# Taking a head's mean off the values instead of off the weighted sums in a retention layer

## The chip, the cores and the metric

The kernel runs on one core of a Trainium2 chip. The metric is the device time of one execution in microseconds (us), as the median of several runs. All data are float32; TensorE is mostly fed with float32r operands, where each number is split into a high part (a cast) and a low part (what the cast left), and a product is made of three matmuls (high by high, low by high, high by low).

## The reference

Two layers, each of a half step (a gated feed-forward with RMS norm), a mixer and a second half step, and a final RMS norm. The input has 512 frames of 1024 features. In the mixer one projection feeds three groups: a convolution (256 features), a stick-breaking attention (8 heads of 64) and a retention (4 heads of 64). What matters here is the retention and the norm over each head's features behind it:

```python
def retention(q, k, v):            # (B, S, H, Dh), Dh = 64
    # weight of key s for query t: gamma_h^|t-s| in the own chunk of 64 frames,
    # gamma_h^(t-s) for earlier chunks, 0 for later ones
    ...
    return (y_intra + y_cross).reshape(B, S, H, Dh)

def head_norm(y, g):
    mu = jnp.mean(y, axis=-1, keepdims=True)
    yc = y - mu
    var = jnp.mean(yc * yc, axis=-1, keepdims=True)
    return (yc * lax.rsqrt(var + EPS)).reshape(B, S, H * Dh) * g

y_r = jax.nn.silu(g_r) * head_norm(retention(rotary(q_r), rotary(k_r), v_r), ret_norm_g)
```

The retention is a sum over keys of weight times value, and the weights are the same for all 64 features of a head. So the mean of y over the features is the same sum over the means of the values.

## The kernel before

The frames lie along the free dimension: a tile is 128 features by 512 frames. The program is not emitted as it is written. Each step is added to a plan as an operation with its engine, an estimated cost, and what it reads and writes. The planner (`Plan.forward`, L192) then runs through estimated time: on each engine it takes, of the operations that are ready, the one with the lowest rank, and that gives a fixed order for each engine. The rank is the operation's place in the program plus shifts: `late` arguments, and the tables `SHIFTS`, by the name of the function that adds it and by the engine. `ORDER` sets the places of the mixer's steps in the program: c (the convolution's inputs), g (gates), i0 to i5 (queries and keys of six pairs of heads; i1 and i4 are the retention's), taps (the convolution), vs and vr (values of the attention and of the retention), a0 to a5 (the pairs' sums), e (the convolution's end), o (the first half of the output product). `DENSE_LATE` puts the large products of the mixer behind the attention's small ones, so that they fill gaps; `TAPS_LATE` puts the 62 taps of the convolution (one VectorE instruction each) behind VectorE's other work. `SPLITS` has a letter for each weight tile: v splits it with a cast on ScalarE and a subtraction on VectorE, d loads it twice, the second time with an accumulating DMA that GpSimd issues.

Tiles come from rooms with a fixed count of slots. A strict room hands its slots out in the order in which the program creates the tiles; a loose one allows others. In PSUM there are three banks for products (`mm`, loose), four for scores (`z`, strict) and one for the sums over keys (`y`, strict). `tiny` has six strict slots for the small columns of norms (`room("tiny", 6)`, L1337).

The retention's way through the code: `values` (L874) multiplies the normalised input by the values' weights, a PSUM bank for two row tiles of 128 frames (the reduction in L894 to L896), and splits each row tile into high (ScalarE, L911) and low (VectorE, L915) with the row's norm factor as scale. `ret_head` (L1039) makes scores (`scores`, L939), multiplies by the decays (L1049), splits, and `weighted` (L957) sums over keys on TensorE (L968). `head_norm` (L1103) then subtracts the mean with one float32 matmul by a constant 128x128 matrix (`centre`, L1106), squares (L1108) and copies back (L1109) on ScalarE, sums the squares by head with small matmuls (L1114), takes the inverse root (`inv_sqrt`, L484), spreads it over the features (L1133) and applies it, the gain and the gate (L1138, L1144). `split_y` (L1062) splits the result for the output product; for the first half of that product the casts wait for the last operation of i5 (L1326).

Of the kernel before, what the change touches and what calls it, by code (L numbers as in the profile page):

```python
# [10 lines left out]
ACT = mybir.ActivationFunctionType  # L11
ALU = mybir.AluOpType
PSUM = bass.MemoryType.PSUM

P = 128
S = 512
# [18 lines left out]
HOLD = 6  # L35


ORDER = "c g i0 taps vs i1 vr a0 a1 i2 i3 a2 i4 a3 a4 i5 a5 e o".split()
SQUARES_LATE = 80

KINDS = "0mffmfe"

SHIFTS = {
    "m": {
        "attend/tensor": -1700, "conv/vector": 505, "inputs": -505, "parts/vector": 5, "ret_head/vector": 80,
        "twice": -10, "twice/vector": 2230, "weight/scalar": 1450, "weight/vector": -10, "weight_by_dma": 410,
        "weights": -3320, "x_ready/scalar": 210,
    },
    "f": {
        "gated/vector": -295, "inner": 435, "inner/tensor": -30, "norm": -180, "parts/scalar": -545,  # L50
        "parts/vector": -1310, "po": -10, "po/tensor": 625, "weight/gpsimd": -430, "x_ready": 395,
    },
    "0": {
        "forms": 1370, "po/tensor": 380, "po/vector": 30, "weight": -1015, "weight/vector": 1300,
        "x_ready/vector": 145,
    },
}


SPLITS = {  # L60
    "0": "vvvvvvvdvvvvvdvdvdvdvvvdvvdvvvvvvdvdvvd",
    "m": "vvdvvvvdvdddvvddvvdvdvvdvdd",
    "f": "dvdvdddddvdvvvddvdvdvdvvvddvvdvvvdvvvvvvdddvvvvddvd",
}

DENSE_LATE, TAPS_LATE = 1140, 1480
PARTS = ((0, 6), (6, 12), (12, 17), (17, 22))
HS = S // 2
TT = S // P
# [280 lines left out]
class Kernel:  # L350
# [520 lines left out]
        return out  # L871

    @group
    def values(self, src, n, cols, out):  # L874

        nc, r = self.nc, self.r
        mm = nc.tensor.matmul
# [22 lines left out]
        for t in range(TT):  # L900
            ps, at = banks[t // share], (t % share) * cols

            for i, tile in enumerate(out[t]):

                def view(tile=tile, ps=ps, at=at + i * HS):
                    parts = tile[:].rearrange("p (h b f) -> p h b f", b=2, f=64)
                    return ps[:, at : at + HS].rearrange("p (h f) -> p h f", f=64), parts[:, :, 0, :], parts[:, :, 1, :]

                def high(t=t, view=view):
                    v, hi, _ = view()  # L910
                    nc.scalar.activation(hi, v, ACT.Copy, scale=r[:, t : t + 1])  # L911

                def low(t=t, view=view):
                    v, hi, lo = view()
                    nc.vector.scalar_tensor_tensor(  # L915
                        out=lo, in0=v, scalar=r[:, t : t + 1], in1=hi.bitcast(F32), op0=ALU.mult, op1=ALU.subtract
                    )

                self.a(HS, high, [ps, r], [(tile, "h")])
                self.v(HS, low, [ps, r, (tile, "h")], [(tile, "l")])  # L920


    BANKS = ((S, ((1, 0), (3, 3 * P))), (2 * P, ((2, 0),)), (S, ((0, 0),)))
# [178 lines left out]
    @group  # L1102
    def head_norm(self, p, y, gain):  # L1103
        nc = self.nc
        ce = self.bank(self.mm, "yce")
        self.pe(0.86, lambda: nc.tensor.matmul(ce[:], self.centre[:], y[:], start=True, stop=True), [self.centre, y], [ce])  # L1106
        sq = self.tile(self.f2, "rsq")
        self.a(S, lambda: nc.scalar.activation(sq[:], ce[:], ACT.Square), [ce], [sq])  # L1108
        self.a(S, lambda: nc.scalar.copy(y[:], ce[:]), [ce], [y])  # L1109
        vs = self.bank(self.mm, "vs")  # L1110

        def sums():
# [156 lines left out]
    def mixer(self, l, after):  # L1269
# [30 lines left out]
        for step in ORDER:  # L1300
            if step[0] in "sa" and self.tables is None:
                self.exp_tables(silus + sigmoids)
            if step == "g":
                silus += self.gates(w_in, banks)
            elif step == "c":
                sigmoids += self.conv_in(w_in, silus, banks)
            elif step == "vs":
                self.vs = [[self.tile(self.r2, "vs", dtype=F32R) for _ in range(2)] for _ in range(TT)]
                self.values(io["m_vs"][l], 2, 512, self.vs)
            elif step == "vr":  # L1310
                self.vr = [[self.tile(self.r2, "vr", dtype=F32R)] for _ in range(TT)]
                self.values(io["m_vr"][l], 4, 256, self.vr)
            elif step[0] == "i":
                self.inputs(int(step[1]), w_in, banks)
                self.last_inputs = len(self.plan.ops) - 1
            elif step[0] == "a":
                self.attend(int(step[1]), rg)
            elif step == "taps":
                self.conv(cw, cb)
            elif step == "o":  # L1320
                self.out_part(w_out, 0)
            elif step == "e":
                self.conv_end(cg, cbeta)
            banks = None
# [6 lines left out]
    def run(self):  # L1331
# [58 lines left out]
            self.v(P, fn, [ones], [t])  # L1390
        self.a(P, lambda: nc.scalar.copy(ident_r[:], ident[:]), [ident], [ident_r])
        self.tri, self.mask = const("tri", [P, P], F32R), const("mask", [P, P], F32R)
        self.blk, self.centre = const("blk", [P, 2]), const("centre", [P, P])
        self.par = {
            n: const(n, [P, DEPTH, *sh])
            for n, sh in (("conv_w", [2, CONV_W]), ("conv_b", [2]), ("conv_ln_g", [2]), ("conv_ln_b", [2]), ("ret_norm_g", [2]))
# [30 lines left out]
def constants():  # L1427
# [6 lines left out]
    diag = np.where(i[:, None] < i[None, :], 0.0, NEG).astype(f)  # L1434
    c["mask"] = diag
    c["blk"] = ((i[:, None] // 64) == (i[None, :] // 64)).astype(f) / f(64)
    c["centre"] = np.eye(P, dtype=f) - c["blk"]
    c["blk"] = np.ascontiguousarray(c["blk"][:, 63:65])
    half = 32
    inv = (f(1.0) / (f(10000.0) ** (np.arange(half, dtype=f) / f(half)))).astype(f)  # L1440
# [61 lines left out]
```

## Time and profile before

| | us |
|---|---|
| median of 3 runs (lowest, highest) | 1919.26 (1919.08, 1924.63) |
| profiled execution | 1922.25 |
| its span, first to last instruction | 1920.5 |
| TensorE busy (matmuls) | 1886.7 |
| VectorE busy | 1325.8 |
| ScalarE busy | 963.0 |
| GpSimd busy | 226.8 |
| DMA, whole span | 301.37 MB |

A profile shows one execution. Busy time of an engine counts its instructions' spans; matmuls overlap each other, so a busy TensorE is not one at its peak. "Granted clock" is the share of full clock that TensorE got. A wait is put down to the instruction that released it last. Tile names appear without their numbers: yce is the centred sum, yr the retention's sum, vr and vs the split values, pv the values' bank, pj a projection's bank, po and mo the output products of a half step and of the mixer, z the scores, y the sums over keys. Mixer 1 runs from about 367 to 614 us, mixer 2 from about 1311 to 1558 us.

### The profile page before, as it was taken

What the parts mean: (1) busy time and instruction counts of PE and PEld (TensorE: products, weight loads), DVE (VectorE), ACT (ScalarE), POOL (GpSimd) and SP (SyncE); (2) the same over time, 40 slices, a digit from 0 to 9 for tenths busy, and PEclk for the clock granted to TensorE, in tenths of its full rate; (3) what the DMA queues carried; (4) which work ended last, traced back from release to release, by engine and by line L of the source; (5) the groups of instructions that cost most, each with busy time, mean ns of one, the idle gap of its engine ahead of it and who ended that gap; (6) DMA issues with size and microseconds to landing.
All of it is one profiled execution on the core that took longest, in us unless ns stands there. A gap on an engine that the chain in (4) does not pass through costs nothing.

```text
span 1920.5 us, 28960 instructions
## 1 busy us (share of the span) xinstructions
PE 1886.7 (98%) x11412; PEld 1683.5 (88%) x11412; DVE 1325.8 (69%) x1921; ACT 963.0 (50%) x1527; POOL 226.8 (12%) x262
## 2 busy tenths in 40 slices
PE   8999999999999999999999999999999999999997
PEld 6899999888878889899889989998888889998995
DVE  6856655699787856566685656657988787564664
ACT  5444444455886534344544444444668765343442
POOL 1011010010102011110211010101111121011100
PEclk9999999999999999999999999999999999999998
DMA  8366675465337577675866676655554385675742
GB/s 249 104 173 180 176 174 155 134 156 139 91 79 197 129 180 193 161 190 161 217 148 163 172 194 170 177 137 142 126 145 121 80 204 138 177 190 154 190 133 79
DMA packets 106344, 301.37 MB, mean 157 GB/s; under 512 B 12384, under 2 KB 13920, under 8 KB 106208
## 3 DMA queue, kind: packets, MB, share of 16 engines
q0 software_dynamic: 43520, 112.74, 30.3%
q1 hardware_dynamic: 62688, 186.78, 30.2%
q8 instruction: 90, 1.47, 0.3%
q14 instruction: 46, 0.38, 0.1%
HBM read 288.98 MB, written 2.10 MB: 152 GB/s over the span
## 4 chain that ended last, share of the span: by engine, by line
PE 82%; DVE 7%; DMA 7%; ACT 2%; issue 1%; SPq 0%; DVEq 0%; POOLq 0%; ACTq 0%
PE po L434 8%; PE po L435 8%; PE po L436 8%; PE pu L662 6%; PE pu L663 6%; PE pu L664 6%; DMA w_raw<-in_f_in 5%; PE pr L663 4%; PE pr L664 4%; PE pr L662 4%; PE pf L434 3%; PE pf L436 3%; PE pf L435 3%; DVE yc L1202 2%; PE pj L434 2%; PE pj L435 2%
## 5 line engine op out<-in xcount | busy, mean ns | idle before, releaser
L379 DVE TENSOR_TENSOR w_lo<-w_raw,w_hi 128x1024 fp32r<-128x1024 f32 (+2 forms) x281 | 313.6, 1117 | 163.8 <-PE po L436 52.4
L376 ACT CAST w_hi<-w_raw 128x1024 fp32r<-128x1024 f32 (+2 forms) x281 | 269.6, 963 | 239.0 <-DVE w_raw L685 69.8
L434 PE MATMUL po<-hh,w_hi 128*128 128x512 f32 x704 | 275.9, 392 | 0.3 <-DVE x L781 0.3
L435 PE MATMUL po<-hl,w_hi 128*128 128x512 f32 x704 | 275.4, 391 | 0.0
L436 PE MATMUL po<-hh,w_lo 128*128 128x512 f32 x704 | 274.0, 389 | 0.0
L662 PE MATMUL pu<-B_hi,w_hi 128*128 128x256 f32 x560 | 158.6, 283 | 4.3 <-DVE up L712 4.3
L662 PE MATMUL pr<-T_hi,s_hi 128*128 128x256 f32 x560 | 157.8, 282 | 0.9 <-ACT ga L699 0.9
L663 PE MATMUL pu<-B_lo,w_hi 128*128 128x256 f32 x560 | 158.4, 283 | 0.0
L664 PE MATMUL pu<-B_hi,w_lo 128*128 128x256 f32 x560 | 158.2, 283 | 0.0
L663 PE MATMUL pr<-T_lo,s_hi 128*128 128x256 f32 x560 | 157.7, 282 | 0.0
L664 PE MATMUL pr<-T_hi,s_lo 128*128 128x256 f32 x560 | 157.6, 281 | 0.0
L436 PEld LDWEIGHTS po<-hh,w_lo 128*128 128x128 f32 x704 | 132.2, 188 | 28.5
L434 PEld LDWEIGHTS po<-hh,w_hi 128*128 128x128 f32 x704 | 132.6, 188 | 24.7 <-DVE x L781 1.2
L677 POOL DMA_DIRECT2D w_raw<-in_f_in x70 | 84.6, 1214 | 583.7 <-DMA w_raw<-in_f_in 418.9
L435 PEld LDWEIGHTS po<-hl,w_hi 128*128 128x128 f32 x704 | 132.7, 188 | 21.9
L404 ACT ACTIVATE w_lo<-w_hi 128x1024 fp32r<-128x1024 f32 (+2 forms) x85 | 79.3, 933 | 96.0 <-DMA w_hi<-in_f_out 30.6
L781 DVE SCALAR_TENSOR_TENSOR x<-po,x 128x512 f32<-128x512 f32 x128 | 87.1, 687 | 51.9 <-PE po L436 51.8
L436 PE MATMUL pf<-xh,w_lo 128*128 128x512 f32 x304 | 118.8, 391 | 0.8 <-DVE w_lo L379 0.8
L434 PE MATMUL pf<-xh,w_hi 128*128 128x512 f32 x304 | 119.5, 393 | 0.0
L435 PE MATMUL pf<-xl,w_hi 128*128 128x512 f32 x304 | 118.7, 390 | 0.0
L725 ACT ACTIVATE ga<-ga 128x512 f32<-128x512 f32 x88 | 55.3, 630 | 121.8 <-DVE ga L719 108.7
L699 ACT COPY ga<-pr 128x256 f32<-128x256 f32 x140 | 51.9, 370 | 125.1 <-PE pr L664 124.7
(216 smaller groups left out, 5037.6 us busy)
## 6 DMA issues: line engine op xcount, KB each, us to landing
w_raw<-in_f_in SPq DMA_DIRECT2D x225, 512.0 KB, 4.7
w_raw<-in_f_in POOLq DMA_DIRECT2D x70, 512.0 KB, 8.0
w_raw<-in_f_out SPq DMA_DIRECT2D x48, 320.0 KB, 3.1
w_raw<-in_f_out SPq DMA_DIRECT2D x38, 384.0 KB, 4.6
w_raw<-in_m_in SPq DMA_DIRECT2D x26, 512.0 KB, 4.4
w_hi<-in_f_out POOLq DMA_DIRECT2D x26, 384.0 KB, 5.2
w_lo<-in_f_out POOLq DMA_DIRECT2D x26, 384.0 KB, 5.0
w_hi<-in_f_in POOLq DMA_DIRECT2D x19, 512.0 KB, 6.0
```

The costliest lines, as they stand in the source:

```text
L376: self.a(n, lambda: nc.scalar.copy(view(hi), view(src)), [src], [hi])
L379: lambda: nc.vector.tensor_tensor(out=view(lo), in0=view(src), in1=view(hi).bitcast(F32), op=ALU.subtract),
L404: self.a(n, lambda: nc.scalar.activation(lo[:, :n], hi[:, :n].bitcast(F32), ACT.Copy, scale=-1.0), [hi], [lo])
L434: mm(acc[:], hi[:, c], h[:], start=first and a + i == 0, stop=False)
L435: mm(acc[:], hi[:, c], l[:], start=False, stop=False)
L436: mm(acc[:], lo[:, c], h[:], start=False, stop=last and a + i == len(ks) - 1)
L662: mm(out, hi[:, c], h, start=first and j + i == 0, stop=False, **opts)
L663: mm(out, hi[:, c], l, start=False, stop=False, **opts)
L664: mm(out, lo[:, c], h, start=False, stop=j + i == 2, **opts)
L677: lambda: nc.gpsimd.dma_start(rs[:].rearrange("p (a b) -> p a b", a=2), src[:, None, 2 * q : 3 * q].to_broadcast([P, 2, q]), accum_op=ALU.add,
L725: self.last_silus = [self.a(S, lambda: nc.scalar.activation(g[:], g[:], ACT.Silu), [g], [g], "silu")]
L781: lambda x=x, po=po: nc.vector.scalar_tensor_tensor(out=x[:], in0=po[:], scalar=-0.5, in1=x[:], op0=ALU.mult, op1=ALU.add),
```

## The change

The centring matmul, its constant and the copy back are gone; the square reads the sum itself. In `values` for the retention, VectorE first sums each head's 64 features of a row tile (four sums a row), and a second instruction adds -1/64 of the sum to the values and writes them to SBUF. The split then reads that tile, where it read PSUM. The sums take a tile of the room `tiny`. With this the order tables change: `ORDER` puts i1 ahead, i0 behind vs and the taps, a2 before i3, i5 before a4, and the output's first half (o) before a5; ranks and splits of weights change in all stages. The letters d go from 10 to 12 of 39 in the first half step, stay 12 of 27 in a mixer, and go from 23 to 20 of 51 in each other half step.

```diff
-ORDER = "c g i0 taps vs i1 vr a0 a1 i2 i3 a2 i4 a3 a4 i5 a5 e o".split()
-SQUARES_LATE = 80
+ORDER = "c g i1 vs taps i0 vr a0 a1 i2 a2 i3 i4 a3 i5 a4 o a5 e".split()
+SQUARES_LATE = 160
...
     "m": {
-        "attend/tensor": -1700, "conv/vector": 505, "inputs": -505, "parts/vector": 5, "ret_head/vector": 80,
-        "twice": -10, "twice/vector": 2230, "weight/scalar": 1450, "weight/vector": -10, "weight_by_dma": 410,
-        "weights": -3320, "x_ready/scalar": 210,
+        "attend": 55, "conv": -50, "conv/vector": 540, "gates": 825, "inputs": -535, "inputs/scalar": -280,
+        "inputs/vector": -210, "out_part": 220, "parts": 450, "parts/scalar": 90, "products/tensor": 340,
+        "project/tensor": 20, "queries": -395, "queries/vector": 390, "spread": 790, "twice/vector": 2385,
+        "values": 175, "weight": -90, "weight_by_dma": 900, "weight_by_dma/scalar": 315, "weights": -2980,
+        "x_ready/scalar": -1075, "x_ready/vector": 280,
     },
     "f": {
-        "gated/vector": -295, "inner": 435, "inner/tensor": -30, "norm": -180, "parts/scalar": -545,
-        "parts/vector": -1310, "po": -10, "po/tensor": 625, "weight/gpsimd": -430, "x_ready": 395,
+        "forms": 100, "gated/vector": -100, "inner": 450, "norm": -970, "parts": -555, "parts/vector": -1070,
+        "po/tensor": 635, "spread/vector": -200, "weight": -970, "weight/scalar": -470, "weight_by_dma": 915,
+        "x_ready": 410,
     },
     "0": {
-        "forms": 1370, "po/tensor": 380, "po/vector": 30, "weight": -1015, "weight/vector": 1300,
-        "x_ready/vector": 145,
+        "first_weights/sync": 530, "forms": 1455, "gate/vector": 1655, "inner/sync": 615, "inner/vector": -590,
+        "norm/tensor": -1565, "parts/scalar": -30, "parts/vector": -915, "pf": 205, "pf/sync": -310, "po": 410,
+        "x_ready": 75,
     },
...
-DENSE_LATE, TAPS_LATE = 1140, 1480
+DENSE_LATE, TAPS_LATE = 960, 1300
...
-    def values(self, src, n, cols, out):
+    def values(self, src, n, cols, out, centred=False):
...
             for i, tile in enumerate(out[t]):
 
+                if centred:
+                    ps, at = self.centred(ps, at), 0
+
...
+    def centred(self, ps, at):
+
+        nc = self.nc
+        m, c = self.tile(self.tiny, "mv", (P, 8)), self.tile(self.f2, "vc", (P, HS))
+
+        def view():
+            return ps[:, at : at + HS].rearrange("p (h f) -> p h f", f=64)
+
+        self.v(
+            HS,
+            lambda: nc.vector.tensor_reduce(out=m[:, :4], in_=view(), axis=mybir.AxisListType.X, op=ALU.add),
+            [ps], [m],
+        )
+
+        def fn():
+            nc.vector.scalar_tensor_tensor(
+                out=c[:].rearrange("p (h f) -> p h f", f=64), in0=m[:, :4, None].to_broadcast([P, 4, 64]),
+                scalar=-1.0 / 64, in1=view(), op0=ALU.mult, op1=ALU.add,
+            )
+
+        self.v(HS, fn, [m, ps], [c], 2)
+        return c
...
     def head_norm(self, p, y, gain):
         nc = self.nc
-        ce = self.bank(self.mm, "yce")
-        self.pe(0.86, lambda: nc.tensor.matmul(ce[:], self.centre[:], y[:], start=True, stop=True), [self.centre, y], [ce])
         sq = self.tile(self.f2, "rsq")
-        self.a(S, lambda: nc.scalar.activation(sq[:], ce[:], ACT.Square), [ce], [sq])
-        self.a(S, lambda: nc.scalar.copy(y[:], ce[:]), [ce], [y])
+        self.a(S, lambda: nc.scalar.activation(sq[:], y[:], ACT.Square), [y], [sq])
         vs = self.bank(self.mm, "vs")
...
-                self.values(io["m_vr"][l], 4, 256, self.vr)
+                self.values(io["m_vr"][l], 4, 256, self.vr, True)
```

## Rows read from the trace of the kernel before

**Rows 1.** The page of the profile, part 1: the span, and busy time, share and instructions of each engine.

```profile
span 1920.5 us, 28960 instructions
...
PE 1886.7 (98%) x11412; PEld 1683.5 (88%) x11412; DVE 1325.8 (69%) x1921; ACT 963.0 (50%) x1527; POOL 226.8 (12%) x262
```

**Rows 2.** Busy time of each engine in six stretches that follow the stages (first half step, mixer 1, two half steps, mixer 2, last half step with the final norm). Columns: stretch, its length, then busy us and instructions of PE, PEld, DVE, ACT and POOL, granted clock (1.00 is full), DMA share, GB/s.

```profile
0.00:367.00 367.00, 362.19 (x2211) 324.45 (x2211) 242.54 (x338) 171.11 (x263) 37.28 (x46) 0.99 0.64 171
367.00:614.00 247.00, 242.28 (x1236) 205.36 (x1237) 204.69 (x330) 164.85 (x278) 31.05 (x35) 0.99 0.53 133
614.00:963.00 349.00, 347.18 (x2247) 317.06 (x2246) 225.32 (x309) 157.57 (x241) 47.10 (x53) 1.00 0.68 174
963.00:1311.00 348.00, 347.33 (x2250) 317.35 (x2250) 225.76 (x309) 157.35 (x240) 40.45 (x48) 1.00 0.64 164
1311.00:1558.00 247.00, 241.70 (x1240) 204.78 (x1239) 205.04 (x332) 164.81 (x280) 31.02 (x35) 1.00 0.54 135
1558.00:1920.50 362.50, 346.03 (x2238) 314.53 (x2237) 222.46 (x306) 147.28 (x227) 39.92 (x45) 0.98 0.58 150
```

**Rows 3.** Who ended TensorE's idle time, whole span. Columns: the instruction that waited, what released it, total us, times, longest us.

```profile
PE pu L662 <- DVE up L712: 4.3, 7, 1.5
PE z L939 <- DVE kk L865: 3.0, 4, 0.9
```

**Rows 4.** TensorE in order of time: the matmuls with idle time before them at the end of mixer 1's projections.

```profile
536.27 0.41 PE L939 MATMUL z<-qh,kk 128*128 128x384 f32 x1 [1.21 <-issue]
...
546.31 0.45 PE L939 MATMUL z<-qh,kk 128*128 128x384 f32 x1 [0.62 <-DVE kk L865]
...
547.85 0.50 PE L434 MATMUL mo<-yh,w_hi 128*128 128x512 f32 x1 [0.57 <-ACT yh L376]
548.70 0.79 PE L435 MATMUL mo<-yl,w_hi 128*128 128x512 f32 x1 [0.35 <-DVE yl L379]
```

**Rows 5.** TensorE's busy time and granted clock around that place, and at the same place of mixer 2. Columns: stretch, its length, busy us and matmuls, granted clock, DMA share, GB/s.

```profile
515.00:548.00 33.00, 30.15 (x161) 1.00 0.60 135
548.00:552.00 4.00, 3.65 (x9) 0.57 0.42 82
1480.00:1500.00 20.00, 18.19 (x98) 1.00 0.48 103
```

**Rows 6.** The instructions on the tile yce (the result of the centring matmul). Columns: line, engine, operation, tile, count: least, median and greatest duration in ns, first and last start in us.

```profile
L1106 PE MATMUL yce<-yr,c_centre x8: 591/592/592, 496.2 to 1506.8; 128*128 128x512 f32 x8
L1108 ACT ACTIVATE rsq<-yce x4: 599/600/602, 497.3 to 1507.4; 128x512 f32<-128x512 f32 x4
L1109 ACT COPY yr<-yce x4: 580/581/583, 497.8 to 1507.9; 128x512 f32<-128x512 f32 x4
```

**Rows 7.** The chain of work that ended last, in mixer 1 around the retention's values and its first head norm. Columns: start us, us, what (merged instructions).

```profile
480.27 0.85 ACT vr L911 x2
...
481.14 0.88 DVE vr L915 x2
...
484.89 1.26 PE y L968 x8
...
496.36 0.86 PE yce L1106 x2
```

**Rows 8.** VectorE's instructions of 400 to 482 us by line and shape. Columns: line, engine, operation, tiles, shapes, count | busy us, mean ns of one | idle time before them.

```profile
L1202 DVE SCALAR_TENSOR_TENSOR yc<-cv,c_conv_w,yc 128x512 f32<-128x512 f32 x45 | 33.7, 749 | 1.0
...
L915 DVE SCALAR_TENSOR_TENSOR vr<-pv,rt,vr 128x256 fp32r<-128x256 f32 x4 | 1.8, 479 | 0.3 <-ACT vr L911 0.2
...
L1049 DVE TENSOR_TENSOR rt<-z,decay 128x256 f32<-128x256 f32 x2 | 0.8, 418 | 0.0
```

**Rows 9.** Busy time by engine in 20 us stretches of mixer 1 (columns as in the six stretches above).

```profile
400.00:420.00 20.00, 19.12 (x88) 15.67 (x87) 19.42 (x30) 12.55 (x19) 3.75 (x5) 1.00 0.77 156
460.00:480.00 20.00, 20.00 (x122) 17.92 (x121) 18.67 (x33) 11.28 (x20) 2.48 (x4) 1.00 0.60 160
```

**Rows 10.** VectorE in order of time in mixer 1: one of the convolution's last taps, and two of the small instructions of its statistics. Columns: start us, us, engine, line, operation, tiles, count [idle before <- releaser].

```profile
479.16 0.74 DVE L1202 SCALAR_TENSOR_TENSOR yc<-cv,c_conv_w,yc 128x512 f32<-128x512 f32 x1
...
491.91 0.16 DVE L490 TENSOR_SCALAR ms<-cvs 128x4 f32<-128x4 f32 x1 [0.48 <-PE cvs L1228]
...
495.08 0.16 DVE L509 TENSOR_TENSOR rt_lo<-rt,rt_hi 128x4 fp32r<-128x4 f32 x1
```

**Rows 11.** ScalarE in order of time at the start of mixer 1: the load of the function table for the exponentials, which follows the second gate's silu.

```profile
406.09 1.28 ACT L1186 ACT_TABLE_LOAD   x1
```

**Rows 12.** TensorE in order of time: the first matmuls of the sums over keys (y) of the five heads that follow the first attention pair. Columns: start us, us, engine, line, operation, tiles, shape, count.

```profile
484.33 0.96 PE L968 MATMUL y<-wh,vr 128*128 128x512 f32 x2
...
491.74 0.65 PE L968 MATMUL y<-wh,vr 128*128 128x512 f32 x2
...
497.57 0.62 PE L968 MATMUL y<-wh,vs 128*128 128x512 f32 x2
...
518.48 0.57 PE L968 MATMUL y<-wh,vs 128*128 128x512 f32 x2
...
530.92 0.56 PE L968 MATMUL y<-wh,vs 128*128 128x512 f32 x2
```

**Rows 13.** TensorE in order of time: the first and the twentieth of twenty matmuls of 512 columns of the projections, with no idle time between them. Columns as in the group of the sums over keys.

```profile
399.65 0.39 PE L435 MATMUL pj<-xl,w_hi 128*128 128x512 f32 x1
...
403.96 0.39 PE L436 MATMUL pj<-xh,w_lo 128*128 128x512 f32 x1
```

More of the change, by code (lines that the diff above doesn't have):

```diff
@@ L60 @@
 SPLITS = {
-    "0": "vvvvvvvdvvvvvdvdvdvdvvvdvvdvvvvvvdvdvvd",
-    "m": "vvdvvvvdvdddvvddvvdvdvvdvdd",
-    "f": "dvdvdddddvdvvvddvdvdvdvvvddvvdvvvdvvvvvvdddvvvvddvd",
+    "0": "vvvvvvvdvdvdvvdvvvvddvvdvvdvdvvvvvddvvd",
+    "m": "vvdvvvvddvddvvddvvdvdvvdvdd",
+    "f": "dvdvdddddvdvvvdvvdvdvdvvvddvvdvvvdvvvvvvdvvvvvvdvdd",
 }
-DENSE_LATE, TAPS_LATE = 1140, 1480
+DENSE_LATE, TAPS_LATE = 960, 1300
 PARTS = ((0, 6), (6, 12), (12, 17), (17, 22))
@@ L1392, in run @@
         self.tri, self.mask = const("tri", [P, P], F32R), const("mask", [P, P], F32R)
-        self.blk, self.centre = const("blk", [P, 2]), const("centre", [P, P])
+        self.blk = const("blk", [P, 2])
         self.par = {
@@ L1436, in constants @@
     c["blk"] = ((i[:, None] // 64) == (i[None, :] // 64)).astype(f) / f(64)
-    c["centre"] = np.eye(P, dtype=f) - c["blk"]
     c["blk"] = np.ascontiguousarray(c["blk"][:, 63:65])
```

## The prediction

> **What bounds the kernel now.** I read the page first, then the stages, then who ended TensorE's waits, then the places of those waits. The page has TensorE busy 98% of the span, VectorE 69%, ScalarE 50% [rows 1]. By stages [rows 2] TensorE stands still 247.00 - 242.28 = 4.7 us in mixer 1 and 5.3 us in mixer 2, 2.5 us in the two half steps between them, 4.8 us in the first half step (mostly before its first data) and 16.5 us in the last stage (mostly the final norm, which has no matmuls to offer). So the kernel is TensorE's own work plus a start and an end that the change hardly touches, and about 10 us of stalls in the mixers. The commonest releaser outside the first half step is VectorE, with a few tenths of a us each time [rows 3]. In mixer 1 the stalls lie where the projections run out [rows 4]: the scores wait 1.21 and 0.62 us, then the output product waits 0.57 and 0.35 us for its operands, because its casts are held until the last projection is split. Behind them the clock is granted at 0.57 of full over 4 us, which means that most of them ran at the lower level of 1.2 GHz; mixer 2 stands still 1.8 us at the same place at full clock [rows 5].
>
> **The centring matmul.** Four of them (two pairs of heads, two mixers), each two instructions [rows 6]. The chain counts 0.86 us for the two [rows 7], so TensorE's work falls by 4 x 0.86 = 3.44 us. TensorE is the path here, so I count it in full; it would be worth less only where TensorE then waits instead. Four copies of 0.58 us leave ScalarE [rows 6] and a bank of PSUM is not taken: ScalarE is half idle, I count nothing. The head norm's chain gets shorter too, but its result is wanted much later. The constant's load leaves SyncE's queue early in the first half step: nothing.
>
> **The centring of the values.** Eight times (four row tiles, two mixers) VectorE gets a tensor_reduce and a scalar_tensor_tensor over 128x256 out of PSUM. No reduce stands in the trace. The nearest rows are operations that read the same shape: 479 ns for the split of vr and 418 ns for a product [rows 8]. A reduce that writes only four elements could be shorter, so the bounds of each are 0.2 and 0.48 us; I take 0.45 us, near both rows. That is 8 x 2 x 0.45 = 7.2 us of VectorE (3.2 to 7.7), 3.6 us for each mixer. ScalarE's and VectorE's split now read SBUF in place of PSUM, and I give them the same price. Where does it lie? VectorE is busy 19.42 and 18.67 of 20 us in the stretches before the retention [rows 9], but much of that, 33.7 us in 82 us, is the convolution's taps [rows 8], which the order leaves for last. So the new work pushes taps, and what it costs TensorE is between nothing and 3.6 us a mixer. I take nothing for the likeliest case, with the far end in the rivals. Below nothing is excluded: these instructions only add work.
>
> The Trainium skill (VectorE: DVE Perf Modes, "Rules for kernel authors") speaks against this part: it calls tensor_reduce the slowest operation of VectorE and advises restructuring where it is on a hot path. In its cost table the reduce has only the plain rate of one element a cycle; an estimate with the page's formula for that rate, (256+151)/0.96, gives 0.42 us, which by the rows is no more than the neighbours' price, so the sum would be the same.
>
> **The wait that comes in.** The values' means take tiles of the room "tiny", six slots handed out strictly in the order in which the program creates them. In the new ORDER the taps stand ahead of vr, so the convolution's four tiny tiles come first: no mean can be taken before the convolution's statistics have run up to their last small subtraction, L509. Before, that one began at 495.08 [rows 10], while vr's last split began at 481.14 and the first sum over keys that uses it followed at 484.89 [rows 7]. Queued behind it are the sums of all later heads (one bank of PSUM, taken in turn) and two of the three product banks, which hold the values. The lowered TAPS_LATE and the new order let the statistics come earlier, or the products of vr later; I take that the planner arranges it so for the likeliest case.
>
> **The new order.** The gates move back by 825 ranks, and the exponentials' table is loaded only behind the gates (406.09 before [rows 11]); the last projections (i5) move ahead of a4, and the first half of the output product ahead of a5. The last two aim where mixer 1 stalls: the held casts come free while attention of two pairs is still to do. What can be had are the waits there (2.75 us), the matmuls at the lower clock (about 4 us at nearly half speed, 1.8 us) and the 1.8 us of mixer 2 [rows 4, 5], 6.3 us together. I take a little over half, 3.6 us; nothing and 6.3 us are the ends for these, and another order may as well open stalls of the same size elsewhere.
>
> **The half steps.** The first gets two more weights by the accumulating DMA, the others three fewer each, which gives VectorE and ScalarE a few us more or less in stages in which TensorE waits 0.7 to 3 us. The cover is the idle time of VectorE, a third of those stages [rows 2]. Without it some of the 4.3 us of waits on "up" [rows 3] would double or go: 0, ends -2 and +3 us.
>
> **The sum.** The profiled execution took 1922.25 us, with a span of 1920.5; the median of the runs is 1919.26, 2.99 lower. 1922.25 - 3.44 - 3.6 = 1915.2, and on the median's footing 1912.2.
>
> **The rivals.**
> (a) Only the matmul's time shows, and the stalls move about: 1919.26 - 3.44 = 1915.8. For it: a list of ranks that is changed everywhere changes stalls both ways. Against it: the stalls at the end of the projections [rows 4] have one cause that the new order touches.
> (b) VectorE's 7.2 us land on TensorE in full, because the splits of the queries and keys already release its waits [rows 3]: 1919.26 - 3.44 + 7.2 = 1923.0; half of it, 1919.4. Against: the taps give way first.
> (c) Slower, by the order of the tiny tiles: if the products of vr stay where they are, its means start at 495.2 and its last tile is ready some 8 x 0.45 + 1 us later, at 500 in place of 482, 18 us late. The following heads' sums stood at 484.3, 491.7, 497.6, 518.5 and 530.9 [rows 12], and need some 6 to 7 us from one to the next, so the gaps before 518.5 and 530.9 swallow 21 us of delay; beyond that every us counts. But for 18 us two of three product banks are held. A projection takes 24 x 0.227 = 5.4 us ((403.96 - 399.65)/19 for one matmul [rows 13]), and with one bank each must be emptied by VectorE (about 1 us) before the next: 3 projections, 3 us. With the convolution 6 us later still, the chain adds another 3 us: 2 x 6 - 3.44 = +8.6, 1927.8. It decides when the means start later than about 498 us. Against: a planner that sees the hold can run vr's products late.
> (d) The retimed order gains nearly all the stalls of the mixers and some of the half steps: 1922.25 - 3.44 - 6.3 - 4 less 2.99, 1905.5.
>
> **How the numbers follow.** Forecast (1908 to 1914.5): 0.48; (a) 0.20; (b) 0.13, of it half above 1919.4; (c) 0.13; (d) 0.06. One measurement of this kernel tells some 0.3%, 5.8 us, from no change: 1913.5 and 1925.0. Of the forecast's case 0.43 lies below 1913.5, with (d) 0.49 faster; (c) less a little is 0.12 slower; the rest, 0.39, within. For 8 in 10 the range goes from 1906 to 1924: it leaves out most of (c) and half of (d).
>
> **What would show it.** Right: no instruction on yce; the reduce at 0.4 to 0.5 us, eight times; mixer stages near 243 us each (247 - 1.7 - 2); the output product starting without its two waits [rows 4]. Wrong: TensorE's waits in the mixers on the split of vr, on the sums, or on VectorE's splits, above 5 us a mixer; the means only behind L509 with y later than 500; gaps ahead of the first exponentials, because the gates come late. A loss or gain above 3 us in the half steps would mean that the ranks, not the centring, made the result.

## The result, and the profile after

The changed kernel is slower: 1928.69 us (median of 9 runs, 1924.11 to 1932.6) against 1921.65 us for the kernel before (9 runs beside it), ratio 1.0038, 95% interval 1.0027 to 1.0049, or 7.0 us. The forecast was a gain, and the range ended at 1924. One execution of the kernel f0 below, 2306.59 us where its other ten took 1913.60 to 1921.67, is in none of the ratios.

The page of the changed kernel, part 1, as [rows 1]:

```profile
span 1929.6 us, 28982 instructions
...
PE 1887.3 (98%) x11404; PEld 1685.9 (87%) x11404; DVE 1332.9 (69%) x1938; ACT 959.3 (50%) x1523; POOL 224.3 (12%) x260
```

TensorE is not less busy than before, although four matmuls of two instructions are gone, and VectorE has 1332.9 - 1325.8 = 7.1 us more. The new instructions, by the tile of the means and by that of the centred values (line, engine, operation, count: least, median and greatest ns, first and last start in us):

```profile
L939 DVE TENSOR_REDUCE mv<-pv x8: 416/418/425, 487.5 to 1442.5; 128x4 f32<-128x256 f32 x8
L944 DVE SCALAR_TENSOR_TENSOR vc<-mv,pv x8: 414/418/422, 488.7 to 1443.3; 128x256 f32<-128x256 f32 x8
L918 ACT ACTIVATE vr<-vc,rt x8: 495/504/511, 490.6 to 1443.8; 128x256 fp32r<-128x256 f32 x8
```

8 x (0.418 + 0.418) = 6.7 us, 0.5 us under the 7.2 us of the prediction. The first five of the six stages, as [rows 2] but with bounds moved to where each stage of this kernel ends:

```profile
0.00:362.00 362.00, 355.96 (x2185) 319.49 (x2186) 235.41 (x330) 167.72 (x258) 39.54 (x49) 1.00 0.66 173
362.00:613.00 251.00, 242.15 (x1238) 206.46 (x1237) 207.49 (x337) 162.91 (x276) 29.51 (x34) 0.99 0.52 127
613.00:963.00 350.00, 346.87 (x2244) 316.64 (x2243) 227.61 (x312) 159.25 (x244) 47.23 (x53) 1.00 0.68 174
963.00:1313.00 350.00, 348.19 (x2246) 317.08 (x2246) 226.95 (x312) 155.54 (x239) 38.37 (x46) 1.00 0.64 164
1313.00:1564.00 251.00, 243.39 (x1243) 207.52 (x1242) 207.22 (x337) 163.55 (x277) 29.47 (x34) 0.99 0.53 128
```

The bounds are the last output product of each stage. By the same mark in both kernels (its last matmul begins at 361.73, 609.70, 957.69, 1306.02, 1552.29 and 1903.60 us before, at 362.22, 613.43, 962.59, 1313.31, 1563.54 and 1912.90 after), the mixers are 3.2 and 4.0 us longer, the two half steps between them 1.2 and 2.4 us, the last one 2.0 us shorter. So most of the loss is where the change is, once in each mixer: 7.2 us of the 9.1 that lie between these two executions (1931.33 and 1922.25 us; the ratio of all runs says 7.0). TensorE stands still 251.00 - 242.15 = 8.9 us in mixer 1 and 7.6 us in mixer 2, 4.7 and 5.3 us before. Who ended those waits in mixer 1 (as [rows 3], of this stage alone; qh and ql are split queries, kk split keys, wt and rt the weights of a pair of heads):

```profile
PE z L969 <- DMA ql<-ql: 2.3, 1, 2.3
PE z L969 <- DVE kk L869: 1.9, 1, 1.9
PE pj L438 <- DVE vs L922: 1.6, 1, 1.6
PE z L969 <- ACT wt L1014: 1.4, 2, 1.0
...
PE z L969 <- DVE rt L1079: 0.6, 1, 0.6
```

The two waits of [rows 4] on the output product's casts (0.57 and 0.35 us) are gone, as the prediction hoped; the last two lines of the list are waits of the scores near that place. The first two lines stand at one place, the first scores of a0, where the kernel before waited only 0.88 us for kk. In order of time:

```profile
449.92 0.44 PE L969 MATMUL z<-qh,kk 128*128 128x384 f32 x1 [1.93 <-DVE kk L869]
452.65 0.69 PE L969 MATMUL z<-ql,kk 128*128 128x384 f32 x1 [2.29 <-DMA ql<-ql]
```

The copies that the second one waits for are issued by SyncE. Its queue around them, and the longest wait of that queue (who waited, on what, total us, times, longest):

```profile
417.95 8.64 SPq L393 DMA_DIRECT2D w_raw<-in_m_in  x2
444.87 0.47 SPq L851 DMA_DIRECT2D qh<-qh  x1
445.44 0.53 SPq L393 DMA_DIRECT2D w_raw<-in_m_in  x1
446.06 0.47 SPq L851 DMA_DIRECT2D qh<-qh  x1
446.63 1.18 SPq L851 DMA_DIRECT2D ql<-ql  x2
449.17 0.33 SPq L393 DMA_DIRECT2D w_raw<-in_m_in  x1
```

```profile
SPq L851 <- ACT qh L840: 18.2, 1, 18.2
```

From 426.59 (417.95 + 8.64) to 444.87 us this queue issues nothing: its entries go out in the order that the plan gave them, the next one is the copy of qh, and qh isn't there yet. When it comes, a weight load of 512 KB is issued among the four copies of 128 KB; another, which GpSimd issued at 442.90, is under way as well. The chain that ended last (start, us, what) runs through it:

```profile
443.50 0.69 DVE q L800
444.19 1.13 DVE w_lo L383
445.32 0.60 DVE ql L843
...
446.63 5.97 DMA ql<-ql
...
452.65 1.01 PE z L969 x3
```

And 4 us stretches (columns as in [rows 2]; the last three are granted clock, DMA share, GB/s):

```profile
440.00:444.00 4.00, 3.64 (x25) 3.18 (x24) 3.86 (x6) 0.00 (x0) 0.55 (x1) 1.00 0.00 0
444.00:448.00 4.00, 3.31 (x18) 2.53 (x18) 3.94 (x7) 2.29 (x3) 0.00 (x0) 1.00 0.83 214
448.00:452.00 4.00, 0.44 (x1) 0.19 (x1) 3.87 (x6) 1.23 (x2) 0.00 (x0) 0.80 1.02 263
452.00:456.00 4.00, 3.35 (x12) 3.16 (x13) 2.44 (x5) 1.92 (x4) 0.00 (x0) 0.50 0.18 49
```

The DMA engines are idle, then busy at 0.83 and 1.02 for 8 us with what is issued at once; TensorE does 0.44 us of work in 4, and the next 4 us are granted 0.50, the lower level of 1.2 GHz. In mixer 2 the same two waits are 1.93 and 1.93 us, and three stretches from 1396 on are granted 0.92, 0.50 and 0.73. VectorE brings q late, since it works off taps first (8 in 6.26 us, from 437.33):

```profile
437.33 6.26 DVE L1229 SCALAR_TENSOR_TENSOR yc<-cv,c_conv_w,yc 128x512 f32<-128x512 f32 x8
443.50 0.69 DVE L800 SCALAR_TENSOR_TENSOR q<-pj,rstd 128x512 f32<-128x512 f32 x1
```

### The profile page after: what moved, and what is told of

Its sections match the earlier page's. It is cut to its first block, busy times and chain, and to the rows that moved or that the text cites. A ratio compares the mean times of both kernels' runs of the same rounds, so it can differ in the third digit from the quotient of the medians.

```text
span 1929.6 us, 28982 instructions
## 1 busy us (share of the span) xinstructions
PE 1887.3 (98%) x11404; PEld 1685.9 (87%) x11404; DVE 1332.9 (69%) x1938; ACT 959.3 (50%) x1523; POOL 224.3 (12%) x260
## 4 chain that ended last, share of the span: by engine, by line
PE 80%; DVE 9%; DMA 7%; issue 2%; ACT 1%; SPq 1%; POOL 0%; DVEq 0%; POOLq 0%; ACTq 0%
PE po L438 8%; PE po L439 8%; PE po L440 8%; PE pu L666 6%; PE pu L668 6%; PE pu L667 6%; DMA w_raw<-in_f_in 4%; PE pr L668 4%; PE pr L667 4%; PE pr L666 4%; PE pf L438 4%; PE pf L439 4%; PE pf L440 4%; DVE yc L1229 3%; DMA sw<-q 2%
## 5 line engine op out<-in xcount | busy, mean ns | idle before, releaser
L439 PE MATMUL pf<-xl,w_hi 128*128 128x512 f32 x304 | 118.9, 391 | 0.0
L440 PE MATMUL pf<-xh,w_lo 128*128 128x512 f32 x304 | 118.9, 391 | 0.0
L666 PEld LDWEIGHTS pu<-B_hi,w_hi 128*128 128x128 f32 x560 | 106.5, 190 | 7.9 <-DVE up L716 4.8
```

The costliest lines, as they stand in the source:

```text
L439: mm(acc[:], hi[:, c], l[:], start=False, stop=False)
L440: mm(acc[:], lo[:, c], h[:], start=False, stop=last and a + i == len(ks) - 1)
L666: mm(out, hi[:, c], h, start=first and j + i == 0, stop=False, **opts)
```

## The experiments

Fifteen kernels. The first four let the planner make a new order; in all later ones the order of every engine is that of the kernel before ("held") or of the changed kernel, but for what is named. Ratios are to the kernel before, run beside them.

**e1, e2: one half of the change each.** e1 has the new code with the old tables, e2 the old code with the new tables.

> The centring moved to the values, with ORDER, SHIFTS, SPLITS and the late constants of before; compared with the kernel before. Theory A (the new tables cost the time: queries and keys of the first pair, i0, come after i1 and vs, so the first scores start at 450 us in place of 412 and TensorE has too little to fill the start of the mixer): the centring alone is a gain of the matmul, -3.4 us, between -1 and -6, and the first scores start near 412. Theory B (the strict room tiny holds two product banks until the convolution's statistics): here too the taps stand ahead of vr, so it is slower than before by 3 to 8 us, with stalls between 480 and 500 us. Theory C (VectorE's 6.7 us of new work lands on TensorE): -3.4 + 3 to 7, 0 to +3 us.

> The arithmetic of before (centring matmul kept) with all new tables; compared with the kernel before. Theory A: slower by the after's +7.0 and the matmul's 3.4, so about +10 us (8 to 13), with the same stalls of TensorE around 430 to 453 us. Theory B: no hold, so within 3 us of before. Theory C: no new work on VectorE, so about +7.0 + 3.4 - 6.7 = +4 us.

Measured: e1 1955.98 us, 1.0182 (1.0164 to 1.0200); e2 1943.54 us, 1.0110 (1.0092 to 1.0128). Either half alone is worse than both together. e1's trace has 12.2 us of waits of the output product for its casts (two, one in each mixer), where the kernel before has 1.1: the planner, given other operations, made another order altogether.

**e3: the means in a room of their own**, so that they needn't come behind the convolution's statistics (rival c).

```diff
-        m, c = self.tile(self.tiny, "mv", (P, 8)), self.tile(self.f2, "vc", (P, HS))
+        m, c = self.tile(self.means, "mv", (P, 8)), self.tile(self.f2, "vc", (P, HS))
...
+        self.means = room("means", 4)
```

> The changed kernel, with the means in a room of their own (four slots), so that they do not wait for the convolution's statistics; compared with the kernel before. Theory A: like the changed kernel, +5 to +9 us, the first scores still start near 450 us. Theory B: the hold goes, and with it what it costs: 0 to -4 us against before. Theory C: like the changed kernel.

Measured: 1951.92 us, 1.0158 (1.0135 to 1.0180).

**e4: i0 ahead again** in the new ORDER.

```diff
-ORDER = "c g i1 vs taps i0 vr a0 a1 i2 a2 i3 i4 a3 i5 a4 o a5 e".split()
+ORDER = "c g i0 vs i1 taps vr a0 a1 i2 a2 i3 i4 a3 i5 a4 o a5 e".split()
```

> The changed kernel with i0 moved ahead in ORDER (c g i0 vs i1 taps vr in place of c g i1 vs taps i0 vr), all other tables as changed; compared with the kernel before. Theory A: the first scores start near 415 to 430 us, the stalls between 430 and 453 us go, and the time falls by 5 to 10 us against the changed kernel, to between -3 and +3 us of before. Theory B: taps and vr stay one after the other, so like the changed kernel, +4 to +9 us. Theory C: like the changed kernel.

Measured: 1964.22 us, 1.0224 (1.0199 to 1.0248). None of the four tells a part of the change apart: each was planned anew, and comes out 24 to 44 us above the kernel before, several times the change itself. They are inconclusive on the parts, and the reason for holding the order from here on.

**f0, f1, f2: the parts alone, order held.** f0 drops the matmul and its copy from the kernel before. f1 has the changed computation: the two instructions of centring stand right ahead of each split, in rooms of their own, and the matmul is gone. f2 has the centring and the matmul. Parts of the edits (the first two lines f0 and f1, the rest f1 and f2):

```diff
-        self.pe(0.86, lambda: nc.tensor.matmul(ce[:], self.centre[:], y[:], start=True, stop=True), [self.centre, y], [ce])
+        self.pe(0.86, lambda: None, [self.centre, y], [ce])
...
+                    if mc:
+                        m = mc[0]
+                        nc.vector.tensor_reduce(out=m[:, :4], in_=v, axis=mybir.AxisListType.X, op=ALU.add)
...
-                    nc.scalar.activation(hi, v, ACT.Copy, scale=r[:, t : t + 1])
+                    nc.scalar.activation(hi, cut(v), ACT.Copy, scale=r[:, t : t + 1])
```

> The kernel before in its own order, with the centring matmul and the copy back left out and nothing put in their place (the mean over a head's features is not taken off at all). Compared with the kernel before. If the matmul's time on TensorE is on the path, as the prediction had it: -3.4 us, -2 to -5. If TensorE then waits instead: 0 to -1.5 us.

> The order of every engine's instructions stays that of before; only the arithmetic changes: the values are centred (the two VectorE instructions stand just ahead of the values' cast, with tiles of rooms of their own), the centring matmul and the copy back are gone. Compared with the kernel before. If the new order alone costs the time (theory A): the matmul's 3.4 us come out as a gain, -1 to -5 us. If VectorE's new work lands on TensorE (theory C): 0 to +4 us.

> As the run before, but the centring matmul and its copy are kept as well, so that only the work on VectorE is added. Compared with the kernel before. Theory A: the centring hides, within 1.5 us of before. Theory C: slower by 3 to 7 us.

Measured: f0 1917.21 us, 0.9983 (0.9970 to 0.9996), 3.3 us faster. f1 1923.79 us, 1.0012 (1.0003 to 1.0022). f2 1925.88 us, 1.0024 (1.0011 to 1.0037), 4.7 us slower. The matmul's price is as predicted. The centring doesn't hide in the order of before: it costs 4.7 us beside the matmul, and f1 less f0 (0.0029 of 1920) is 5.6 us. f1 and f0 were not run side by side, but their intervals don't meet.

**k1: f1 with 8 of 62 taps less in each mixer; d0: the kernel before with 8 taps less.**

```diff
                 def fn(j=j, y=y, cv=cv, c=c):
+                    if j >= CONV_W - 4:
+                        return
```

> The kernel before in its own order with the same 8 taps left out in each mixer (part of the convolution is left out). Theory D: in this order TensorE hardly waits for VectorE behind the taps, so it gains less than 3 us. If VectorE is what bounds every mixer: it gains 6 to 12 us as well.

> The kernel before with its order held fast, the values centred and the matmul left out, and of the convolution 8 of 62 taps of a mixer left out as well, so that VectorE has about 6 us less to do in each mixer against the 3.3 us that centring adds. Theory Q (centring costs TensorE because VectorE has that much more to do): the time comes down to that of the kernel without matmul and without centring, ratio 0.998 to 0.999. Theory L (each split of the values is ready 0.84 us later, four times in a row, and what follows on the queues of all engines waits, whatever VectorE has to do elsewhere): it stays at 1.001 to 1.002, since 8 taps fewer alone gave nothing (0.9999).

Measured: d0 1919.85 us, 0.9999 (0.9988 to 1.0011); k1 1920.02 us, 0.9989 (0.9980 to 0.9998). Fewer taps give nothing to the kernel before, and 4.4 us (0.0023) to the one that centres. So centring costs by VectorE's load (theory Q): in a held order its 3.3 us in each mixer push all that stands behind on VectorE's queue, and where as much is taken off that queue elsewhere, the cost goes. To the splits being late (theory L) the remaining 1.2 us are left, which the intervals don't tell from nothing. The traces agree: the last of ScalarE's casts of the values begins 121.8 and 122.2 us behind the half step's last matmul in f1, 118.9 and 118.9 in f0, and in k1, at 121.2 and 121.0, it is still some 2 us late.

**d1: the changed kernel with 8 taps less in each mixer.** The rival for the place at 450 us: VectorE alone is late, and the copies don't matter.

> The changed kernel in its own order, but each of the convolution's two columns leaves out its last 4 of 31 taps, so VectorE has 8 x 0.78 = 6.2 us less in each mixer (part of the convolution is left out). Compared with the kernel before. Theory D (the taps run at 0.77 us where the plan counts 0.69, so VectorE falls some 5 us behind the plan by the first scores, and the new order has TensorE wait for it): the stalls before the first scores shrink to a third, and the time falls by 7 to 14 us against the changed kernel, to -7 to 0 us of before. If TensorE waits there for the transfers of the queries' other half, or for banks, and not for VectorE: at most 3 us fall, +4 to +7 us.

Measured: 1928.04 us, 1.0042 (1.0029 to 1.0056): nothing gained. Its first scores, of mixer 1:

```profile
PE z L969 <- DMA ql<-ql: 3.8, 1, 3.8
PE z L969 <- DVE kk L869: 1.9, 1, 1.9
```

q comes 3.4 us earlier (440.06 in place of 443.50; 0.8 of it because this mixer began earlier), and the wait for the copy grows from 2.3 to 3.8 us: the copies of ql now take 7.4 us from issue to landing, 5.9 in the changed kernel. VectorE's lateness by itself falls as the cause.

**h2: the weight load behind the four copies**, once in each mixer; nothing else is moved. **h2d1**: the same with 8 taps less.

```diff
+        for ids in self.together:
+            at = [k for k, o in enumerate(order) if o.i in ids]
+            loads = [o for o in order[at[0] : at[-1]] if o.engine == "sync" and o.i not in ids]
+            last = order[at[-1]]
+            order = [o for o in order if o not in loads]
+            k = order.index(last) + 1
+            order[k:k] = loads
...
```

> The changed kernel; in SyncE's queue alone the one weight load that stands among the four copies of i0's queries to the other half of the partitions is put behind them, in each mixer. Compared with the kernel before. Theory E (the copies stand ahead of weight loads in SyncE's queue and wait 18 us for the queries; once released they share the DMA engines with the load of 512 KB, so the last lands 6 us after its issue and the first scores wait for it): the copy lands 3 to 4 us after its issue, the scores' wait for it falls from 2.3 and 1.9 us to under 1, with less time at the lower clock, and the time falls by 3 to 7 us against the changed kernel: -1 to +4 us of before. If the copies are slow by themselves: no change, +5 to +9 us.

> As the run before, and 8 taps of the convolution left out in each mixer (part of the convolution is left out). Theory E with theory D as its first half (VectorE's lateness holds the queue, the load behind it holds the copies): with both gone the first scores wait only for the split of the keys, and the time falls by 8 to 14 us against the changed kernel, -7 to -1 us of before. If the start of the attention is not what made the change slower: within 3 us of the changed kernel.

Measured: h2 1920.86 us, 0.9998 (0.9988 to 1.0009); h2d1 1919.75 us, 0.9999 (0.9988 to 1.0010). The order of one load against three copies is worth 0.0040, 7.7 us (some 3 either way by the intervals), as much as the change had lost. h2d1 was expected 8 to 14 us below the changed kernel and comes out level with h2: with the load behind the copies too, fewer taps give nothing that shows. SyncE's queue in h2, and then its first scores:

```profile
443.53 1.13 SPq L860 DMA_DIRECT2D qh<-qh  x2
444.76 1.19 SPq L860 DMA_DIRECT2D ql<-ql  x2
446.04 2.13 SPq L401 DMA_DIRECT2D w_raw<-in_m_in  x2
```

```profile
448.59 0.44 PE L978 MATMUL z<-qh,kk 128*128 128x384 f32 x1 [1.94 <-DVE kk L878]
448.87 0.34 PE L978 MATMUL z<-ql,kk 128*128 128x384 f32 x1
```

The wait for kk stays, the one for ql is gone. From issue to landing the copies of ql take, in the changed kernel and then in h2:

```profile
DMA to landing us min/median/max: 5.8/5.9/6.0
```

```profile
DMA to landing us min/median/max: 2.8/3.0/3.2
```

The mixers of h2 are 247.9 and 244.8 us long by the mark of the output product, 251.2 and 250.2 in the changed kernel. In the traces the place itself accounts for it: from the first matmul of these scores to the first of the next step (z<-lh,r_tri) the two mixers take 12.63 (449.92 to 462.55) and 12.59 us in the changed kernel, 9.55 (448.59 to 458.14) and 7.98 in h2, 3.1 + 4.6 = 7.7 us less. The waits for ql are 2.29 + 1.93 = 4.2 of that; the rest is the same work done faster, with less time below full clock (in mixer 2 of h2 the granted clock stays at 1.00).

**h5: h2 with 8 taps moved behind the split of i0's keys**, so that queries and keys come earlier.

> The changed kernel with the load behind the copies and, on VectorE, the 8 taps that stand ahead of i0's queries, and those among its splits, moved behind the split of i0's keys in each mixer; nothing is left out. Compared with the kernel before. Theory E: the queries are ready some 6 us sooner, the first scores start near 446 us in place of 452.7, and the time falls by 8 to 14 us against the changed kernel, -7 to -1 us of before, so this version would beat both. If the taps are missed later as much as they are saved here (the statistics, and behind them the values' means, come 6 us later): 0 to 4 us fall, +3 to +7 us.

Measured: 1927.65 us, 1.0038 (1.0026 to 1.0051), 7.7 us slower than h2. The first scores begin at 443.28 in place of 448.59 and no longer wait; the next step of the same head does, in mixer 1 and in mixer 2 (3.50 us there too):

```profile
454.82 0.79 PE L1070 MATMUL z<-lh,r_tri 128*128 128x512 f32 x1 [3.50 <-ACT lh L400]
456.43 0.79 PE L1070 MATMUL z<-ll,r_tri 128*128 128x512 f32 x1 [0.81 <-DVE ll L403]
```

This wait is of the edit's own making. That step needs the tile sp, which VectorE has to finish, and VectorE first works off 14 taps without a break, the moved ones and those that stood behind them:

```profile
442.52 10.99 DVE L1255 SCALAR_TENSOR_TENSOR yc<-cv,c_conv_w,yc 128x512 f32<-128x512 f32 x14
```

The alternative's size is about right (+3 to +7 us), its reason is not: the means start at 483.16, as in h2 (483.12). What earlier queries are worth without this hold, h5 doesn't show.

**g2: h2 without any centring.** **g1: h2 with two operations of the half step ahead of the sums of squares**, which wait 1.36 us for VectorE behind each mixer. Parts of the edits (first line g2, the rest g1):

```diff
-            lambda: nc.vector.tensor_reduce(out=m[:, :4], in_=view(), axis=mybir.AxisListType.X, op=ALU.add),
...
+        for i in self.behind:
+            here = next(k for k, o in enumerate(order) if o.i == i)
+            nxt = [o for o in order[here + 1 :] if o.engine == "tensor"][:2]
...
```

> The changed kernel with the weight load behind the copies; VectorE's two instructions for the means are left out, and the splits read the values' bank, so that nothing at all is centred (no matmul either). All else in the same order. If the centring costs as much in the new order as in the old (4.7 us beside its matmul, 5.6 without): ratio 0.9970 to 0.9975, some 1915. If it hides in the new order, which has given the taps' room to it: 0.9990 to 1.0000, no less than the kernel with the load behind the copies had (0.9998).

> The changed kernel with the weight load behind the copies, and in the half steps behind the mixers two operations of the up projection (three matmuls each) stand ahead of the sums of squares that wait for VectorE 1.36 us. Computes all of the reference. If the stall there and the lower clock behind it are a loss of their own, two of them give back 2 x 1.4 us and most of 2 x 1.7 us at the lower level: ratio 0.9965 to 0.9980, faster than both kernels. If the wait only turns up behind the two operations, at the next sums: 0.9990 to 1.0000.

Measured: g2 1921.9 us, 1.0004 (0.9995 to 1.0013), no faster than h2: in the new order the centring costs nothing that the times show (h2 less g2 is -0.0006, within 0.0014). The traces leave a us or two open: the mixers are 245.0 and 245.3 us long in g2, 247.9 and 244.8 in h2, 247.8 and 247.5 in g1, which centres in the order of h2. g1 1920.11 us, 0.9990 (0.9981 to 0.9998): the wait is gone from its trace, but of the expected 0.0018 to 0.0033 against h2 only 0.0008 came, and the two intervals overlap. Of the versions that leave nothing out it is the fastest; its 1.9 us under the kernel before are less than the 0.3% that the prediction counts as told from no change.

## Why the prediction was wrong

**The matmul: right.** 3.44 us predicted, 3.3 measured (f0).

**The centring: right in its size, half right in its cost.** 6.7 us of VectorE for the predicted 7.2. The reduce measures 418 ns. That is the 0.42 us which the prediction estimated with a formula of the Trainium skill (VectorE: DVE Perf Modes, "The TRN2 errata", where it stands for an add of two tensors); the warning in its "Rules for kernel authors", that tensor_reduce is the slowest operation, is not borne out in this shape, where the scalar_tensor_tensor takes 418 ns too. That the taps give way and TensorE pays nothing holds in the new order, as far as the times show (g2 against h2). In the order of before it doesn't: 4.7 to 5.6 us (f2, f1), between the 3.6 and 7.2 us of rival (b), and by the mechanism that (b) names, VectorE's load (k1). f1 comes out within the 1919.4 to 1923.0 of (b), carried to the footing of the prediction: 1919.26 x 1.0012 = 1921.6.

**The wait that comes in (rival c): there, and harmless.** The first means stand right behind the convolution's last small subtraction, as (c) said:

```profile
487.46 0.16 DVE L513 TENSOR_TENSOR rt_lo<-rt,rt_hi 128x4 fp32r<-128x4 f32 x1
487.54 0.42 DVE L939 TENSOR_REDUCE mv<-pv 128x4 f32<-128x256 f32 x1
```

That is 487.5 us, below the 498 us from which (c) decides, and TensorE doesn't stand still behind it (nor from 1412 to 1472 us, at the same place of mixer 2):

```profile
460.00:480.00 20.00, 20.00 (x113) 17.06 (x113) 15.93 (x27) 16.21 (x30) 1.42 (x2) 1.00 0.26 49
480.00:500.00 20.00, 20.00 (x129) 18.29 (x128) 18.45 (x38) 16.97 (x33) 2.65 (x3) 1.00 0.42 117
500.00:520.00 20.00, 20.00 (x117) 17.66 (x116) 16.87 (x32) 18.21 (x36) 2.62 (x2) 1.00 0.43 99
```

The slower result is not (c)'s: that (c) has the same sign, and with 1927.8 us nearly the size, is coincidence.

**The new order: the step that failed.** The prediction took "a little over half" of 6.3 us as a gain, 3.6 us, with "nothing and 6.3 us" as the ends (its 1.8 us for the lower clock is 1.7 by [rows 5], which changes little), and gave the other direction ("another order may as well open stalls of the same size elsewhere") neither a bound nor a rival. With centring at nothing, as the prediction has it, the new order measures 7.0 + 3.3 = 10.3 us of loss. It looked at the end of the projections. There the waits on the casts did go and no stretch falls below full clock, but the scores wait instead: in all TensorE stands still there for 2.75 and 2.28 us before, 1.97 and 3.31 us after. And it did not look at the place where ORDER moves the most: i0, the first pair's queries and keys, from third place to sixth, behind vs and the taps. That touches three queues, and none was costed. On VectorE the taps come ahead of q. In SyncE's queue the copies of qh and ql wait at the head, from 427 to 445 us, with the weight loads behind them. And then the transfer engines get everything at once, with a load in front of the copies that TensorE waits for. Before, the same copies were issued some 10 us before the first scores, with no load among them (SyncE's queue, then TensorE):

```profile
400.37 1.17 SPq L847 DMA_DIRECT2D qh<-qh  x2
401.75 2.37 SPq L847 DMA_DIRECT2D ql<-ql  x2
```

```profile
412.03 0.44 PE L939 MATMUL z<-qh,kk 128*128 128x384 f32 x1 [0.88 <-DVE kk L865]
```

**The sum as measured.** Against the kernel before: the matmul -3.3 us (f0); centring in the new order about 0 (g2 against h2); the load among the copies 0.0040, 7.7 us (h2 against the changed kernel). -3.3 + 7.7 = 4.4 of 7.0 us. The remaining 2.6 us are the rest of the new order, as g2 says from the other side: with nothing to centre and the load put right it takes 1.0004, f0 in the old order 0.9983, some 4 us apart. The interval of each of these differences is some 3 us, so the rest is barely told from nothing. The split depends on the order in which the parts are added: with the same centring in both, the changed kernel against f1, the new order costs 0.0026, 5.0 us. Stage by stage the profiled executions put the rest outside the mixers: g2's mixers are 245.0 and 245.3 us long, f0's 245.4 and 245.4, while the half steps behind the mixers are 3.6 and 1.8 us longer in g2. Behind mixer 1 this is no accident of one execution: the half step takes 349.2 to 351.0 us in six traces with the order of the changed kernel, 346.7 to 348.6 in six with the order of before; the other half steps overlap. The sums of squares behind each mixer wait for VectorE in the new order, and didn't before (behind mixer 1, before and after):

```profile
614.06 0.94 PE L553 MATMUL ss<-ones,sq 128*128 128x1 f32 x8
```

```profile
617.22 1.02 PE L557 MATMUL ss<-ones,sq 128*128 128x1 f32 x8 [1.36 <-DVE sq L483]
```

g1, which takes up this wait, has 347.1 us in that half step; in the whole time it got back 1.5 us, which the intervals don't tell from nothing. What the rest is, ranks or the letters of SPLITS, was not tried apart.

**The half steps** were bounded at -2 and +3 us together with a likeliest value of 0; by the marks above they lose 0.5 + 1.2 + 2.4 - 2.0 = 2.1 us, within the bounds, on the dearer side.

## What to carry to other kernels

When an order is changed, follow each moved step down every queue that it uses, the one that issues its DMAs first: a small copy that waits at the head of an ordered queue holds the loads behind it, and then has to share the transfer engines with what was held. An instruction added to an engine that is 69% busy is not hidden by the mean: in one fixed order it cost TensorE about 5 of its 6.7 us, in another nothing that the times show, so the price belongs to the order and is measured with the order held. And parts of a change to a planned kernel can be told apart only with the order held; replanned, each of the four variants was worse than the whole.

## What the runs showed of the hardware

The two copies of ql (128 KB each, within SBUF) took 5.9 us from issue to landing in mixer 1 and 5.5 us in mixer 2 with a load of 512 KB issued 1.2 us ahead of the first of them, and 3.0 and 2.3 us with the same load issued behind them (a load of 512 KB by GpSimd was issued some 2 us before the four copies, in both kernels and both mixers). The Trainium skill (DMA: Bandwidth & Descriptors, "Two DMAs through the same engine are not ordered") says that within one queue of a transfer engine the descriptors start in order; the two traces agree with that, as the copies issued behind the load land 2.9 us later. Whether the place in the queue or the shared engines make the difference, no run here shows.

Waits of 1.93 and 2.29 us, with 0.44 us of work between them, were followed by 4 us granted at 0.50 and 4 at 0.84, while TensorE had work again from 452.65 on. In h2 a wait of 1.94 us at the same place was followed by 0.74 and 0.83 in mixer 1; in mixer 2 one of 1.92 us was followed by 1.00.
